# Layer norm with GELU: statistics in groups of three tiles that match the transfer blocks, one tile in three on ScalarE

## The chip, the cores and the metric

The kernel runs on one core of a Trainium2 chip. The metric is the device time of one execution in microseconds (us), and a time given for a kernel is the median of its runs. Executions of one kernel scatter by 0.5 to 2.6 us here. Comparisons are made by ratio, with a 95% interval. PE is the matrix engine, DVE VectorE, ACT ScalarE, POOL GpSimd, SP the engine whose queue issues the large transfers.

## The reference

```python
# x: (8, 1024, 2048) f32, gamma and beta: (2048,), eps = 1e-5
mean = np.mean(x, axis=-1, keepdims=True)
var = np.var(x, axis=-1, keepdims=True)
normalized = (x - mean) / np.sqrt(var + eps)
out = gamma * normalized + beta
return 0.5 * out * (1 + np.tanh(np.sqrt(2 / np.pi) * (out + 0.044715 * out ** 3)))
```

The 8192 rows are 64 tiles of 128 rows; a tile is 1.05 MB. All of x comes in once and a result of the same size goes out: 134.22 MB.

## The kernel before

Tiles travel in blocks: tile 0 alone, then 21 blocks of three tiles (3.15 MB a transfer; the first of these comes in, and the last goes out, tile by tile). Seven block buffers form a ring; the result overwrites x in its buffer. A load waits for the store that last used its buffer.

```python
starts = [0] + list(range(1, ntiles, R))          # R = 3, blocks 0 to 21
groups = [1, 1, 2] + [4] * 14 + [2, 1, 1]         # tiles that share one POOL chain
on_scalar = {first[g] for g, size in enumerate(groups) if size == 4}   # 14 tiles

def chunk(i, c):                                  # statistics of a quarter tile on DVE
    ...bn_stats; after the 4th quarter bn_aggr
def scalar_mean(i): ...                           # ACT pass over the tile, sums x
def scalar_var(i):  ...                           # ACT pass, sums (x - mean)^2; POOL scales it
def group_chain(g):                               # POOL: 1/sqrt(var + eps) by three Newton steps
    ...                                           # 15 tiny operations, each needs the one before
def diagonal(j):                                  # ACT: w = ident * std, one per tile
def affine(j):                                    # per half: DVE writes (x - mean) * gamma to PSUM,
    ...                                           # PE adds w^T beta on top (needs diagonal(j))
def gelu(j):                                      # per half: ACT gelu(PSUM / std) -> x's buffer
    ...                                           # last tile of a block: store(b), load(b + 6)

for j in range(ntiles):
    g, k = of_tile[j]
    target = min(len(chunks), max(pos + GAP, done_at[g] + SLACK))   # GAP, SLACK = 3, 7
    while pos < target:
        ...chunk(i, c)                            # where a group is complete: its chain
    if k == 0:
        for q in range(groups[g]):
            diagonal(j + q)
    affine(j)
    if j > 0:
        gelu(j - 1)
    ...                                           # then perhaps one ACT statistics pass
```

PSUM has room for two tiles' products, so `affine(j)` waits for `gelu(j - 2)`.

## Time and profile before

| before | value | how to read it |
|---|---|---|
| time | 322.51 us (322.26 to 322.91, 3 runs) | span in the profile 320.9 us |
| DVE, ACT, POOL, PE busy | 88, 67, 38, 81% | an average, not a proof of a bound |
| x in, result out on the DMA engines | 98.2% of the span | the candidate for the bound |

The waits between engines show how few of DVE's there were, and what ACT waited for. The columns are total us, times, longest; `...` marks lines left out here and below:

```profile
ACT xt L179 <- PE ps L170: 59.3, 62, 6.0
...
ACT w L161 <- POOL std L155: 26.6, 15, 5.6
DVE st L124 <- DMA xt<-in_x_dram: 18.3, 6, 4.7
...
DVE ps L167 <- ACT xt L179: 1.9, 5, 0.4
```

Only x made DVE wait noticeably; ACT waited mostly for products from PE, and in 15 places for the end of a POOL chain.

### The profile page before, as it was taken

To read this page: it belongs to the slowest core of one execution; us is meant where nothing else is said; L and a number is where in the kernel's file an instruction comes from. 1 tells how busy PE (TensorE), PEld (TensorE's weight loads), DVE (VectorE), ACT (ScalarE), POOL (GpSimd) and SP (SyncE) were. 2 spreads that over 40 slices of the span, in tenths; PEclk is the share of its full clock that TensorE was granted. 3 is DMA by queue.
4 is the path that set the end of the run, shared out by engine and by line. 5 is a ranking of instruction groups with operands and counts; after the bars stand their busy time and mean duration, and the time that the engine had idled before them with its cause. 6 is when DMAs were issued, how large, how long until landed. Compare 5 with 4: busy or idle time off the path is not lost.

```text
span 320.9 us, 2333 instructions
## 1 busy us (share of the span) xinstructions
PE 259.1 (81%) x528; PEld 102.8 (32%) x528; DVE 284.0 (88%) x379; ACT 215.7 (67%) x254; POOL 120.7 (38%) x319
## 2 busy tenths in 40 slices
PE   6988399888888888887499888748988859888990
PEld 2333144333333333333143333213333323333430
DVE  3999999999999999979499999849999979999830
ACT  3248399979787777775648787761978774655751
POOL 0771506080615334260301707030071532658840
PEclk9999869999999999997879999996999998999998
DMA  7999999999999999999999999999999999999597
GB/s 296 452 417 435 439 405 407 434 423 432 426 435 432 423 429 418 434 432 433 432 420 438 436 438 432 414 437 438 432 438 425 417 441 438 435 425 433 245 425 312
DMA packets 7074, 134.38 MB, mean 419 GB/s; under 512 B 786, under 2 KB 786, under 8 KB 1042
## 3 DMA queue, kind: packets, MB, share of 16 engines
q1 hardware_dynamic: 7056, 134.22, 98.2%
q8 instruction: 4, 0.07, 0.1%
q14 instruction: 10, 0.08, 0.1%
q10 hardware_dynamic: 4, 0.02, 0.0%
HBM read 67.13 MB, written 67.11 MB: 418 GB/s over the span
## 4 chain that ended last, share of the span: by engine, by line
DMA 49%; DVE 24%; POOL 12%; issue 8%; PE 2%; ACT 2%; POOLq 0%; SPq 0%; DVEq 0%; ACTq 0%
DMA out_dram<-xt 26%; DMA xt<-in_x_dram 23%; DVE ps L167 12%; DVE st L124 11%; POOL t L152 3%; POOL y L154 2%; POOL t L153 2%; PE ps L170 2%; POOL t L151 2%; ACT xt L179 1%; DVE mv L126 1%; POOL std L155 1%; POOL y L148 1%; POOL ve L147 1%; ACT w L161 0%
## 5 line engine op out<-in xcount | busy, mean ns | idle before, releaser
L170 PE MATMUL ps<-b_t,w 128*128 128x512 f32 x512 | 245.1, 628 | 51.6 <-DVE ps L167 43.8
L179 ACT ACTIVATE xt<-ps,y 128x1024 f32<-128x1024 f32 x128 | 139.3, 1107 | 60.0 <-PE ps L170 59.3
L170 PEld LDWEIGHTS ps<-b_t,w 128*128 128x128 f32 x512 | 97.6, 199 | 199.8 <-issue 100.9
L167 DVE SCALAR_TENSOR_TENSOR ps<-xt,mv,g_t 128x1024 f32<-128x1024 f32 x128 | 157.6, 1276 | 1.9 <-ACT xt L179 1.9
L124 DVE BATCH_NORM_STATS2 st<-xt 128x6 f32<-128x512 f32 x200 | 125.8, 672 | 18.4 <-DMA xt<-in_x_dram 18.3
L137 POOL TENSOR_SCALAR mv<-sq 128x1 f32<-128x1 f32 x14 | 3.8, 268 | 101.8 <-ACT junk L135 101.8
L161 ACT ACTIVATE w<-ident,std 128x128 f32<-128x128 f32 x64 | 20.8, 390 | 26.6 <-POOL std L155 26.6
L152 POOL TENSOR_TENSOR t<-t,ve 128x4 f32<-128x4 f32 (+2 forms) x60 | 35.3, 589 | 4.7
L147 POOL TENSOR_SCALAR ve<-mv 128x4 f32<-128x4 f32 (+2 forms) x20 | 4.6, 229 | 62.6 <-DVE mv L126 62.2
L135 ACT ACTIVATE junk<-xt,mv 128x2048 fp8e5<-128x2048 f32 x14 | 27.9, 1994 | 0.0
L153 POOL TENSOR_SCALAR t<-t 128x4 f32<-128x4 f32 (+2 forms) x60 | 25.4, 423 | 5.3
L130 ACT ACTIVATE junk<-xt 128x2048 fp8e5<-128x2048 f32 x14 | 26.6, 1901 | 0.0
L151 POOL TENSOR_TENSOR t<-y 128x4 f32<-128x4 f32 (+2 forms) x60 | 23.0, 383 | 4.8
L154 POOL TENSOR_TENSOR y<-y,t 128x4 f32<-128x4 f32 (+2 forms) x60 | 16.5, 276 | 5.0
L126 DVE BATCH_NORM_AGGREGATE mv<-st 128x2 f32<-128x24 f32 x50 | 13.2, 264 | 2.8
L97 PE MATMUL ps<-g_t,ones 1*128 1x512 f32 x8 | 7.2, 1072 | 2.6 <-DMA g_t<-in_gamma_dram 2.6
L97 PE MATMUL ps<-b_t,ones 1*128 1x512 f32 x8 | 7.0, 1056 | 0.0
L155 POOL TENSOR_TENSOR std<-ve,y 128x4 f32<-128x4 f32 (+2 forms) x20 | 5.9, 293 | 1.6
L148 POOL TENSOR_SCALAR y<-ve 128x4 int32<-128x4 int32 (+2 forms) x20 | 5.8, 289 | 1.7
L100 ACT ACTIVATE g_t<-ps 128x1024 f32<-128x1024 f32 x2 | 2.0, 1023 | 5.7 <-PE ps L97 5.7
L100 ACT ACTIVATE b_t<-ps 128x1024 f32<-128x1024 f32 x2 | 2.0, 1023 | 4.8 <-PE ps L97 4.8
L97 PEld LDWEIGHTS ps<-g_t,ones 1*128 1x128 f32 x8 | 2.5, 325 | 5.7 <-issue 5.7
(11 smaller groups left out, 10.4 us busy)
## 6 DMA issues: line engine op xcount, KB each, us to landing
xt<-in_x_dram SPq DMA_DIRECT2D x20, 3072.0 KB, 21.9
out_dram<-xt SPq DMA_DIRECT2D x20, 3072.0 KB, 27.1
xt<-in_x_dram SPq DMA_DIRECT2D x4, 1024.0 KB, 8.3
out_dram<-xt SPq DMA_DIRECT2D x3, 1024.0 KB, 18.6
out_dram<-xt SPq DMA_DIRECT2D x2, 512.0 KB, 5.5
g_t<-in_gamma_dram ACTq DMA_DIRECT2D x1, 8.0 KB
b_t<-in_beta_dram ACTq DMA_DIRECT2D x1, 8.0 KB
```

Source lines behind the costliest of these rows:

```text
L97: nc.tensor.matmul(pt[:, c:c + BANK], lhsT=ones[0:1, :], rhs=row[0:1, s.start + c:s.start + c + BANK], start=True, stop=True)
L124: nc.vector.bn_stats(out=sts[i][:, c, :], in_=xts[i][:, c * BANK:(c + 1) * BANK])
L130: nc.scalar.activation(out=junk, in_=xts[i], func=ACTF.Identity, scale=-1.0 / d, accum_out=slot(i)[:, 0:1], saturate=False)
L135: nc.scalar.activation(out=junk, in_=xts[i], func=ACTF.Square, bias=slot(i)[:, 0:1], accum_out=sq, saturate=False)
L151: po.tensor_tensor(out=t, in0=y, in1=y, op=MUL)
L152: po.tensor_tensor(out=t, in0=t, in1=ve, op=MUL)
L153: po.tensor_scalar(out=t, in0=t, scalar1=-0.5, scalar2=1.5, op0=MUL, op1=ADD)
L154: po.tensor_tensor(out=y, in0=y, in1=t, op=MUL)
L161: nc.scalar.activation(out=w, in_=ident, func=ACTF.Identity, scale=rstds[g][1][:, k:k + 1])
L167: nc.vector.scalar_tensor_tensor(out=pt, in0=xts[j][:, s], scalar=mvs[g][:, k, 0:1], in1=g_t[:, s], op0=ADD if j in on_scalar else SUB, op ...
L170: nc.tensor.matmul(pt[:, c:c + BANK], lhsT=wts[j], rhs=b_t[:, s.start + c:s.start + c + BANK], start=False, stop=True, skip_group_check=True)
L179: nc.scalar.activation(out=xts[j][:, s], in_=pt, func=ACTF.Gelu_apprx_tanh, scale=rstds[g][0][:, k:k + 1])
```

## The change

The groups become equal to the blocks, each group's first tile has its statistics on ScalarE (21 tiles instead of 14), and the distance between statistics and products is set by position in the group. This takes work off VectorE, the busiest engine, and lets a group of products end where a store begins.

```diff
-    GAP, SLACK = 3, 7
-    groups = [1, 1, 2] + [4] * 14 + [2, 1, 1]
+    groups = [1] + [3] * ((ntiles - 1) // 3)
-    on_scalar = {first[g] for g, size in enumerate(groups) if size == 4}
+    on_scalar = {first[g] for g, size in enumerate(groups) if size == 3}
+    AFTER = (6, 9, 11)
-        target = min(len(chunks), max(pos + GAP, done_at[g] + SLACK))
+        target = min(len(chunks), max(pos, done_at[g] + AFTER[k]))
-        if passes and of_tile[passes[0][1]][0] <= now and (j + 1 == ntiles or of_tile[j + 1][1]):
+        if passes and of_tile[passes[0][1]][0] <= now and k != 1:
```

## The prediction

> **What bounds the kernel now.** I read four views in this order: the busy lines and slices of the page, the DMA queue table, the waits of the queue that issues the transfers, and a table of stretches of the last 25 us.
>
> ```profile
> PE 259.1 (81%) x528; PEld 102.8 (32%) x528; DVE 284.0 (88%) x379; ACT 215.7 (67%) x254; POOL 120.7 (38%) x319
> ...
> DVE   3999999999999999979499999849999979999830
> ...
> DMA   7999999999999999999999999999999999999597
> GB/s 296 452 417 435 439 405 407 434 423 432 426 435 432 423 429 418 434 432 433 432 420 438 436 438 432 414 437 438 432 438 425 417 441 438 435 425 433 245 425 312
> ...
> q1 hardware_dynamic: 7056, 134.22, 98.2%
> ```
>
> DVE looks like the bound at 88%, but the DMA row has a 9 in every slice but four: the first, and 297 to 305 us and after. The queue that carries x in and the result out holds the 16 DMA engines 98.2% of the span. 134.22 MB must move whatever the kernel computes. The busy share of DVE is high because its work nearly fits the transfers' time, not because it sets it.
>
> ```profile
> SPq L71 <- DMA out_dram<-xt: 184.9, 15, 15.1
> SPq L187 <- ACT xt L179: 80.5, 10, 18.0
> ```
>
> The issuing queue waits 184.9 us for stores to land before it may load into their buffers (15 loads, all the later ones): the ring of seven buffers is full, and transfers, not arithmetic, pace it. From 106 to 254 us the stretch table of that time has the DMA share at 1.00 to 1.01 and 429 to 430 GB/s. Only the tail shows transfers waiting for arithmetic:
>
> ```profile
> 296.00:300.00 4.00, 4.00 (x10) 1.71 (x9) 3.84 (x4) 2.23 (x2) 3.59 (x6) 1.00 0.90 387
> 300.00:304.00 4.00, 4.00 (x11) 1.75 (x10) 3.15 (x3) 2.78 (x4) 3.51 (x7) 1.00 0.29 123
> 304.00:308.00 4.00, 4.00 (x11) 1.85 (x10) 3.04 (x3) 1.96 (x2) 3.44 (x7) 1.00 1.09 461
> 308.00:312.00 4.00, 3.34 (x8) 1.26 (x8) 0.00 (x0) 2.88 (x4) 0.76 (x4) 1.00 0.88 375
> 316.00:321.00 5.00, 0.00 (x0) 0.00 (x0) 0.00 (x0) 0.00 (x0) 0.00 (x0) 0.73 0.59 238
> ```
>
> The last two numbers of a line are DMA share and GB/s, the others busy times of PE, weight loads, DVE, ACT, POOL. From 300 to 304 us the DMA share is 0.29: the store of block 20 is issued only at 303.16 us, after the GELU of tile 60. That looks like a hole of some 3 us. But each transfer has sixteen shares, one per DMA engine, and the trace records each share's completion. The store of block 19 (3.15 MB) completes its first share at 299.82 us and its last at 304.36. The slowest share was still busy when the next store came at 303.16, so on that engine there was no hole. Its last completions are 289.87, 297.12, 304.36 (7.25 us a block), then 311.88, 314.34 and 316.88 for block 20 and tiles 61 and 62, and 319.44 for the second half of tile 63. After 304.36 a pure 7.25 us a block would give 304.36 + 2 x 7.25 = 318.86. So the visible hole of 3 us cost the slowest share only 319.44 - 318.86 = 0.6 us.
>
> **What the Trainium skill says.** "Perfetto Trace Analysis", section Roofline: a single core may pull more than its 358 GB/s share of memory, but is bounded by its 16 DMA engines at about 435 GB/s. The trace agrees: 429 to 430 GB/s over the middle, 3.1457 MB in 7.25 us = 434 GB/s on the slowest share. "DMA: Bandwidth & Descriptors", section Latency and other measured facts: some DMA engines are usually slower than the others (the cause given there is a guess, for another way of issuing). Here the completions of one block are spread by 4.5 us late in the run; which engines these are I did not find. "SBUF — State Buffer", section SBUF: two separate sides: DVE and GpSimd share a port pair as an exclusive lock, the loser waits out the instruction. The trace agrees: the same small POOL operations last 0.20 us, and about 1.1 us in many places where DVE runs the two-input product (from 291.64 to 301.14 us a chain of 15 took 9.5 us, in the quiet start 25.53 - 21.44 = 4.1 us).
>
> **The change part by part.**
>
> ```profile
> L179 ACT ACTIVATE xt<-ps,y 128x1024 f32<-128x1024 f32 x128 | 139.3, 1107 | 60.0 <-PE ps L170 59.3
> ...
> L167 DVE SCALAR_TENSOR_TENSOR ps<-xt,mv,g_t 128x1024 f32<-128x1024 f32 x128 | 157.6, 1276 | 1.9 <-ACT xt L179 1.9
> L124 DVE BATCH_NORM_STATS2 st<-xt 128x6 f32<-128x512 f32 x200 | 125.8, 672 | 18.4 <-DMA xt<-in_x_dram 18.3
> ```
>
> First figure after the bar: busy time of the group; I divide that by the count, since neighbours overlap.
>
> (1) Seven more tiles (21, not 14) have statistics on ScalarE. DVE loses 7 x (4 x 125.8/200 + 13.2/50) = 7 x 2.78 = 19.5 us: 284.0 becomes about 264.5. ACT gains 7 x (1.90 + 1.99 + 2 x 0.19 for reading the sums) = 7 x 4.28 = 30 us: 215.7 becomes about 246.
>
> (2) 22 groups instead of 20: two more POOL chains of 15 operations, 120.7/20 = 6.0 us each, and seven more scalings: POOL about 135 us, under half the span.
>
> (3) Transfers, bytes, buffers and their issue order on the queue are unchanged; the instruction listing of both kernels shows the same 38 rows there.
>
> Per block of three tiles DVE then needs 2 x 2.78 + 6 x 157.6/128 = 5.56 + 7.39 = 12.95 us (before, averaged, 13.9), ACT 6 x 1.09 + 3 x 0.33 + 4.28 = 11.8 us, PE 24 products at about 0.46 = 11.1 us. A load and a store of a block need 2 x 7.25 = 14.5 us. All engines stay below that; before they were below it too. So 19.5 us off DVE lie wholly beside transfers: DVE will wait longer for x, nothing else.
>
> (4) Start. The first 19 tiles are loaded without a condition; the slowest share ends them at 50.7 us, the store of tile 0 at 53.95. Only then (its buffer) can load 7 go out. In the new order the second store needs tile 9's first half: block 3 has landed by 28.1, and 20.8 (block 2) + 14 chunks at 0.695 + 4 products at 2.46 + about 4 us for PE and GELU = 44 us. That is before 52, so no hole; gain 0.
>
> (5) Tail. The last loads land at 260.80 and 275.33 us. In the new DVE order, after the wait at 260.8: 8 chunks, 2 aggregates and 3 products (12.95 us) to 273.8, wait to 275.3, 8 chunks, 2 aggregates and 3 products to 288.3. Tile 61's second scalar pass ends near 288.4, then one POOL chain of about 9 us instead of three in a row: 297.5, diagonals 298.5, GELU of tile 60 to about 300.7. Store 19 goes out near 286 (before 290.75), store 20 near 301 (before 303.16). Then PE paces: 3.7 us a tile after 298.3, so tiles 61, 62, 63 leave near 303, 307 and 310.5 (before 306.59, 311.49 and 314.38). The fast shares' hole shrinks to about 1 us, the slowest share has none and ends at 318.9 instead of 319.44. **Gain about 0.6 us.**
>
> Sum: 322.51 - 0.6 = **321.9 us**.
>
> **Rivals.** (a) The hole counts in full: the slowest share speeds up once others have less to do. The missing shares of 296 to 304 us are 0.1 x 4 + 0.71 x 4 = 3.2 us, with the end up to 4 us: about 318.5 us. Against it: when the fast shares stopped at 299.8, the slow one kept its 7.24 us a block. (b) A new wait: ScalarE's queue now puts the mean of a block not yet landed, and diagonals that wait for a POOL chain, ahead of the third tile's GELU, and that GELU frees the PSUM half that DVE needs. From the end of a block's statistics to the product that needs this half DVE has about 9 x 0.63 + 0.26 + 2 x 2.46 = 10.8 us; a chain under contention (8 to 9.5) with diagonals and half a GELU needs 10 to 12. If it costs 1.2 us a block DVE comes to 14.2 us, still under 14.5; if it costs 3, 15 blocks lose 1.5 us each, and the time is 345. Speaks against it: chains only take that long when DVE is not waiting, and the ring holds a block ahead. (c) DVE was the true bound: 19.5 us less would give 303 us; against it, 134.22 MB at 434 GB/s are 309 us by themselves.
>
> **Range and chances.** The three times before lie within 0.7 us. The slowest share loses some 6 us over the run in short delays I cannot attribute (one load took 8.7 us instead of 7.3 near 125 us); these may shift by 1 us either way. With (a) in part below and a little of (b) above: 320.5 to 323.3. Faster by over 2% means below 316.1, less than the transfers leave: 0.01. Slower by over 2% needs (b) at full size: 0.03. Within 2%: 0.96.
>
> **What would show it right or wrong.** Right: DVE busy near 264.5 and ACT near 246; DVE's wait for x above 30 us instead of 18.3; DMA still 9 in the middle slices and 98% or more on the queue; the share in the hole near 300 us rises from 0.29 to above 0.6, with the span shorter by less than 1.5 us. Wrong: 6s or 7s in the middle of the DMA row (rival b), products waiting for ScalarE by tens of us; or a span under 318 (rival a).

## The result, and the profile after

The changed kernel took 322.12 us (321.52 to 322.72, 4 runs) against 322.71 us (322.26 to 323.08, 4 runs) for the kernel before in the same rounds. Ratios in this document are the mean time of one kernel's runs over that of the other's in the same rounds, so not quite the ratio of the medians; here 0.9982, with a 95% interval of 0.9959 to 1.0006.

The page's busy lines and slices of the changed kernel:

```profile
PE 253.1 (79%) x528; PEld 104.0 (33%) x528; DVE 269.1 (84%) x344; ACT 238.6 (75%) x282; POOL 149.6 (47%) x356
...
DVE   2677799999999999999999999999999989798420
...
DMA   7999999999999999999999999999999999999797
GB/s 297 442 427 440 440 406 397 430 439 424 440 421 431 431 437 437 418 434 423 437 434 424 434 434 427 433 427 437 422 443 421 428 441 427 439 418 431 308 424 315
...
q1 hardware_dynamic: 7056, 134.22, 98.4%
```

DVE lost 15 us of work, ACT gained 23, and the DMA row differs from the one before in a single slice (7 instead of 5, at 297 to 305 us). The waits tell where the freed time went:

```profile
SPq L186 <- ACT xt L178: 154.0, 16, 23.6
SPq L70 <- DMA out_dram<-xt: 125.0, 14, 14.2
...
ACT w L160 <- POOL std L154: 49.9, 21, 6.4
DVE ps L166 <- ACT xt L178: 21.1, 37, 4.3
...
DVE st L123 <- DMA xt<-in_x_dram: 12.1, 5, 4.9
```

The queue now waits more for GELU results (154.0 us, before 80.5) and less for stores to land (125.0, before 184.9). DVE waits less for x, and 21.1 us for ScalarE to free PSUM, instead of 1.9. So the stores of the first half leave **later** in the changed kernel, although its busiest engine has less to do: block 2 at 61.00 us instead of 55.45, block 6 at 114.34 instead of 106.18, block 11 at 181.03 instead of 180.31. The tail, in stretches of 4 us (last two numbers: DMA share, GB/s; the others as in the prediction's table of this kind):

```profile
296.00:300.00 4.00, 1.42 (x4) 0.39 (x3) 0.62 (x1) 1.08 (x4) 2.23 (x9) 1.00 0.89 381
300.00:304.00 4.00, 4.00 (x11) 1.81 (x10) 3.06 (x3) 3.80 (x4) 0.00 (x0) 1.00 0.64 270
304.00:308.00 4.00, 4.00 (x10) 1.71 (x9) 1.82 (x2) 2.46 (x3) 0.00 (x0) 1.00 0.95 406
308.00:312.00 4.00, 1.94 (x5) 0.57 (x3) 0.00 (x0) 2.23 (x2) 0.00 (x0) 1.00 0.95 399
```

In the hole at 300 to 304 us the DMA share rose from 0.29 to 0.64, yet the end moved by only 1.2 us in this pair of profiles.

**A new loop.** ACT's and POOL's instructions in order of time (start, duration, engine and line; in brackets the idle time before, and what ended it) show one block period of the changed kernel. First POOL, the beginning of a chain, its end, and the next beginning:

```profile
129.72 0.22 POOL L136 TENSOR_SCALAR mv<-sq 128x1 f32<-128x1 f32 x1 [5.09 <-ACT junk L134]
...
137.77 0.20 POOL L154 TENSOR_TENSOR std<-ve,y 128x3 f32<-128x3 f32 x1
143.06 0.22 POOL L136 TENSOR_SCALAR mv<-sq 128x1 f32<-128x1 f32 x1 [5.09 <-ACT junk L134]
```

Then ACT between the two chains:

```profile
138.00 0.98 ACT L160 ACTIVATE w<-ident,std 128x128 f32<-128x128 f32 x3 [2.46 <-POOL std L154]
138.89 2.10 ACT L178 ACTIVATE xt<-ps,y 128x1024 f32<-128x1024 f32 x2
140.89 1.99 ACT L134 ACTIVATE junk<-xt,mv 128x2048 fp8e5<-128x2048 f32 x1
142.78 0.19 ACT L134 ACTIVATION_READ_ACCUMULATOR junk<-xt,mv 128x1 f32 x1
```

A chain ends (137.97). ACT makes the diagonals that waited for it, then the GELU behind them in its order, then the variance pass of the next block; only that lets the next chain begin. 8.25 (chain, with the scaling of the variance in front) + 0.03 + 0.89 (diagonals) + 2.00 (GELU) + 2.08 (variance) + 0.09 = 13.34 us, and 143.06 - 129.72 = 13.34. The stores of blocks 2 to 10 are issued at 61.00, 74.34, 87.67, 101.01, 114.34, 127.68, 141.01, 154.35 and 167.69 us: the same 13.34 us apart. The loop, not VectorE and not yet the transfers, paces the stores there; from 194 to 253 us each store goes out right behind a load, 14.5 to 15.0 us apart; by 261.04 us (block 17) the stores are back on the loop's count. The DMA engines do not run dry in all this (share 1.00 from 61 to 254 us), since the ring holds work ahead.

The questions for the experiments were therefore three. Do the transfers alone explain the time? How near is this loop to costing time? And where do the 0.6 us come from?

### The profile page after: what moved, and what is told of

It is laid out like the page before. It is cut to its first block, busy times and chain, and to the rows that moved or that the text cites. A ratio compares the mean times of both kernels' runs of the same rounds, so it can differ in the third digit from the quotient of the medians.

```text
span 319.7 us, 2374 instructions
## 1 busy us (share of the span) xinstructions
PE 253.1 (79%) x528; PEld 104.0 (33%) x528; DVE 269.1 (84%) x344; ACT 238.6 (75%) x282; POOL 149.6 (47%) x356
## 3 DMA queue, kind: packets, MB, share of 16 engines
q1 hardware_dynamic: 7056, 134.22, 98.4%
## 4 chain that ended last, share of the span: by engine, by line
DMA 34%; POOL 30%; issue 26%; PE 3%; ACT 2%; DVE 1%; POOLq 0%; SPq 0%; ACTq 0%
DMA out_dram<-xt 26%; POOL t L152 10%; DMA xt<-in_x_dram 8%; POOL y L153 6%; POOL t L151 6%; PE ps L169 3%; POOL t L150 3%; ACT xt L178 2%; POOL mv L136 1%; POOL std L154 1%; POOL ve L146 1%; DVE st L123 1%; POOL y L147 1%; ACT w L160 1%; DVE ps L166 0%
## 5 line engine op out<-in xcount | busy, mean ns | idle before, releaser
L169 PE MATMUL ps<-b_t,w 128*128 128x512 f32 x512 | 239.1, 625 | 53.3 <-ACT w L160 52.4
L166 DVE SCALAR_TENSOR_TENSOR ps<-xt,mv,g_t 128x1024 f32<-128x1024 f32 x128 | 158.7, 1287 | 21.1 <-ACT xt L178 21.1
L178 ACT ACTIVATE xt<-ps,y 128x1024 f32<-128x1024 f32 x128 | 134.4, 1107 | 9.6 <-PE ps L169 8.9
L123 DVE BATCH_NORM_STATS2 st<-xt 128x6 f32<-128x512 f32 x172 | 109.5, 670 | 12.1 <-DMA xt<-in_x_dram 12.1
L160 ACT ACTIVATE w<-ident,std 128x128 f32<-128x128 f32 x64 | 21.1, 391 | 49.9 <-POOL std L154 49.9
L152 POOL TENSOR_SCALAR t<-t 128x3 f32<-128x3 f32 (+1 forms) x66 | 50.7, 767 | 5.8
L134 ACT ACTIVATE junk<-xt,mv 128x2048 fp8e5<-128x2048 f32 x21 | 41.9, 1993 | 0.1
L129 ACT ACTIVATE junk<-xt 128x2048 fp8e5<-128x2048 f32 x21 | 40.2, 1916 | 0.0
L153 POOL TENSOR_TENSOR y<-y,t 128x3 f32<-128x3 f32 (+1 forms) x66 | 32.2, 488 | 5.5
L151 POOL TENSOR_TENSOR t<-t,ve 128x3 f32<-128x3 f32 (+1 forms) x66 | 31.2, 473 | 5.2
L150 POOL TENSOR_TENSOR t<-y 128x3 f32<-128x3 f32 (+1 forms) x66 | 14.8, 224 | 5.3
L146 POOL TENSOR_SCALAR ve<-mv 128x3 f32<-128x3 f32 (+1 forms) x22 | 5.2, 235 | 9.1 <-DVE mv L125 7.4
L154 POOL TENSOR_TENSOR std<-ve,y 128x3 f32<-128x3 f32 (+1 forms) x22 | 5.2, 237 | 1.7
(11 smaller groups left out, 13.4 us busy)
```

The source lines that it names most:

```text
L123: nc.vector.bn_stats(out=sts[i][:, c, :], in_=xts[i][:, c * BANK:(c + 1) * BANK])
L129: nc.scalar.activation(out=junk, in_=xts[i], func=ACTF.Identity, scale=-1.0 / d, accum_out=slot(i)[:, 0:1], saturate=False)
L134: nc.scalar.activation(out=junk, in_=xts[i], func=ACTF.Square, bias=slot(i)[:, 0:1], accum_out=sq, saturate=False)
L150: po.tensor_tensor(out=t, in0=y, in1=y, op=MUL)
L151: po.tensor_tensor(out=t, in0=t, in1=ve, op=MUL)
L152: po.tensor_scalar(out=t, in0=t, scalar1=-0.5, scalar2=1.5, op0=MUL, op1=ADD)
```

## The experiments

Twelve runs, all correct but the first, which is wrong. Each ratio is to the kernel before, run in the same rounds. The difference shown is against the changed kernel unless said. "Store 20" is the store of block 20, the last full block, as its issue time in the trace.

### 1. Transfers alone

The loop over the tiles is replaced by the loads and stores in the same order on the same queue, as soon as data and buffers allow.

```diff
-    for j in range(ntiles):
-        ...  (statistics, products, GELU, stores)
+    for j in range(ntiles):
+        store(j)          # the same stores; after store(b) the load of block b + 6
```

> All loads and stores of the changed kernel, in the same queue, order and sizes, with no statistics, products or GELU on the tiles (the result is x itself, wrong on purpose). Theory (the slowest of the 16 DMA shares sets the end): 320.5 to 322.5 us, within 0.5% of both kernels, last shares of the blocks about 7.25 us apart. Rival (arithmetic still costs some us through waits for buffers or late stores): below 318 us.

Measured: 321.63 us (320.63 to 322.51), ratio to before 0.9967 (0.9946 to 0.9989). The page of this run:

```profile
PE 14.0 (4%) x16; PEld 5.1 (2%) x16; DVE 0.2 (0%) x1; ACT 5.6 (2%) x6; POOL 0.5 (0%) x5
...
DMA   7999999999999999999999999999999999999993
...
q1 hardware_dynamic: 7056, 134.22, 98.1%
```

With 0.2 us of VectorE work the kernel takes the same time to 0.3%. This is the floor of the transfers as they are arranged; the kernel before stands 0.3% above it (interval 0.1 to 0.5%), the changed kernel 0.1 to 0.2%, which is within the scatter. The spread between the first and last share of a block is there too (block 19: first share complete at 299.33 us, last at 303.96), so it does not come from the arithmetic.

### 2. A store in the tail sent earlier

```diff
+        early = k == 0 and g == len(groups) - 1
+        if early:
+            gelu(j - 1)               # tile 60, ahead of the last diagonals
         if k == 0: ...diagonals
-        if j > 0:
+        if j > 0 and not early:
             gelu(j - 1)
```

> The changed kernel with one move in the tail: the GELU of tile 60 comes ahead of the last group's diagonals on ScalarE, so the store of block 20 is issued near 297 to 298 us instead of 301.94. Theory (the slowest share alone counts, and it had no hole): DMA share 300 to 304 us rises from 0.64 to 0.8 or more, time as the changed kernel within 0.3 us (321.8 to 322.4). Rival (the hole counts in full for all shares): 2 to 3 us less, about 319.5 us.

Measured: 322.29 us, ratio 0.9987 (0.9970 to 1.0004). Store 20 left at 297.38 us, and the stretch table of its tail has the hole at 300 us filled:

```profile
296.00:300.00 4.00, 0.20 (x1) 0.00 (x0) 2.52 (x3) 1.11 (x1) 3.35 (x9) 0.79 0.97 418
300.00:304.00 4.00, 3.42 (x4) 1.50 (x5) 0.00 (x0) 0.99 (x3) 0.10 (x1) 0.50 1.00 430
304.00:308.00 4.00, 4.00 (x9) 1.73 (x8) 1.57 (x2) 2.23 (x2) 0.00 (x0) 0.86 0.81 350
308.00:312.00 4.00, 4.00 (x11) 1.76 (x10) 1.01 (x1) 2.50 (x3) 0.00 (x0) 1.00 0.74 307
```

The share at 300 to 304 us is 1.00 instead of 0.64 and the time did not fall; block 20's slowest share ended at 311.48 us here against 310.85 in the changed kernel's profile. But the hole has moved to 304 to 312 us rather than closed: from 296 to 312 us the missing shares add up to 1.9 us, in the changed kernel to 2.3. So this run alone does not rule out that the hole counts in full; runs 1 and 7, which have none, do.

### 3. Only the tail undone

```diff
-    groups = [1] + [3] * ((ntiles - 1) // 3)
+    groups = [1] + [3] * 20 + [1, 1, 1]
```

> The changed kernel with only its tail undone: tiles 61, 62 and 63 are three groups with one chain each and all statistics on VectorE, as before. Theory: the gain of the change sits in the tail, so this gives it back: the last half tile's store is issued near 314 us instead of 311.1, and the time is 0.3 to 1 us above the changed kernel (322.4 to 323.1). Rival (the gain is chance in the middle of the run): the same as the changed kernel, 322.1 within 0.2 us.

Measured: 321.94 us, ratio 0.9980 (0.9960 to 1.0000); the same as the changed kernel. The last store did leave late, at 315.12 us (near 314 expected), and it gave nothing back that can be measured. But this edit does not restore the old tail: tile 61's chain now stands alone, and the store of block 20 left at 299.34 us, not at 303.16 as in the kernel before or at 301.94 as in the changed one. So the run shows that a late last store costs nothing; it does not test whether the late store 20 of the kernel before did.

### 4 and 5. A longer chain, in both kernels

```diff
-        for _ in range(3):            # in group_chain
+        for _ in range(5):
```

> The changed kernel with five steps of the inverse square root instead of three: eight more operations in each POOL chain, nothing else. Theory (a loop of chain, diagonals, one GELU and the next variance pass, 13.34 us a block, runs just below the 14.5 us of a block's transfers): the loop grows by 8 operations of 0.28 to 0.6 us to 15.6 to 18 us a block, above the transfers, and the time to 350 to 390 us, with the stores issued at that spacing. Rival (the chain is hidden beside VectorE's 12.95 us and the transfers): 322 to 326 us, only the tail later.

> The kernel before with five steps of the inverse square root instead of three. Theory: the same loop exists there, but once per four tiles: about 8.3 us of chain, 1.3 of diagonals, 2.1 of GELU, 2.2 of variance pass, 14 us against 19.4 us of transfers for four tiles; with 2.2 to 5 us more it stays below, so the middle keeps its pace and only the tail's three chains are later: 323 to 330 us. Rival (a longer chain hurts both kernels alike): as the changed kernel with five steps, 350 us or more.

Measured: the changed kernel 366.87 us, ratio 1.1368 (1.1347 to 1.1390); the kernel before 339.25 us, ratio 1.0526 (1.0508 to 1.0543). The first hit the theory: a chain of 10.4 us instead of 8.25 and stores 15.53 us apart (15.6 to 18 expected). The second missed its range of 323 to 330 us, though the loop there did stay below the transfers: chains began at 150.97, 169.47 and 187.98 us, 18.5 us per four tiles against 19.4 (13.9 per three tiles against 14.5). A loop below the transfers' pace was not enough. That led to the next theory, and to run 9.

### 6. The longer chain with the loop cut

```diff
-        for _ in range(3):
+        for _ in range(5):
...
-        if passes and of_tile[passes[0][1]][0] <= now and k != 1:
-            f, q = passes.pop(0)
-            f(q)
+        for _ in range(2 if k == 2 else 0):      # mean and variance pass back to back,
+            if passes and of_tile[passes[0][1]][0] <= now:      # ahead of the diagonals
+                f, q = passes.pop(0)
+                f(q)
```

> The changed kernel with five steps, and the variance pass of a block put right behind its mean pass on ScalarE, ahead of the previous block's diagonals and GELU. That cuts the loop: a chain no longer waits for what the chain before released. Theory: the spacing of the stores falls from 15.6 to 18 us to the larger of VectorE's 13 us, ScalarE's 12 us and POOL's own chain (11 to 13 us), below the transfers' 14.5: time 322 to 327 us. Rival (the longer chain itself is what costs, not the loop): within 2% of the changed kernel with five steps alone.

Measured: 331.48 us, ratio 1.0279 (1.0241 to 1.0318). 35 of the 45 us came back by moving one pass, so the loop, not the chain's length by itself, was most of the cost. But it is above the expected 322 to 327 us: the stores are still 13.7 us apart, and the first block's leaves at 52.00 us instead of 47.66.

### 7. A shorter chain

```diff
-        for _ in range(3):
+        for _ in range(1):
```

> The changed kernel with one step instead of three (the inverse root is less exact, on purpose): eight operations fewer in each chain. Theory: the loop shrinks to 9 to 11 us, the product's waits for ScalarE on VectorE (21.1 us) fall below 8 us, VectorE's wait for x grows from 12 to over 25 us, and the time stays at 321.5 to 322.5 us since transfers set it. Rival (the loop costs time before the ring of buffers is full): below 319 us.

Measured: 322.41 us, ratio 0.9999 (0.9982 to 1.0015). DVE's waits in this run:

```profile
DVE st L123 <- DMA xt<-in_x_dram: 29.5, 14, 4.6
...
DVE ps L166 <- ACT xt L178: 3.4, 2, 2.1
```

With the loop this much shorter the wait for ScalarE turns into a wait for x, and no time is won. In the changed kernel the loop costs nothing that these runs can measure. The tail of this run has no hole either: from 296 to 312 us its DMA shares are 0.93, 1.07, 0.92 and 1.00.

```profile
300.00:304.00 4.00, 4.00 (x11) 1.77 (x10) 3.20 (x3) 2.59 (x4) 0.00 (x0) 1.00 1.07 455
304.00:308.00 4.00, 3.32 (x8) 1.14 (x6) 0.00 (x0) 2.79 (x3) 0.00 (x0) 1.00 0.92 393
```

So closing the hole all but some 0.3 us is worth no measurable time, which rules out that it counts in full.

### 8. All statistics on VectorE

```diff
-    on_scalar = {first[g] for g, size in enumerate(groups) if size == 3}
+    on_scalar = {first[g] for g, size in enumerate(groups) if size == 0}
```

> The changed kernel with no statistics on ScalarE: all 64 tiles on VectorE. Theory: VectorE then needs 3 x 2.78 + 7.39 = 15.7 us a block, above 14.5, and sets the time: 21 x 15.7 plus about 15 us of start and end = 340 to 350 us, VectorE busy above 95%. Rival (VectorE's share has no bearing at all): 322 to 325 us.

Measured: 356.76 us, ratio 1.1062 (1.1045 to 1.1078); 7 us above the expected range, and DVE was 90% busy, not over 95%. The stores were at first 15.1 us apart, later 15.1 and 15.6 in turn. With groups of three, statistics on ScalarE are needed; how few tiles would do was not tried.

### 9. One step more: a loop just below the transfers

```diff
-        for _ in range(3):
+        for _ in range(4):
```

> The changed kernel with four steps of the inverse square root: four more operations in each chain. Three and five steps gave stores 13.34 and 15.53 us apart, so four give about 14.4 us, below the 14.5 us of a block's load and store. Theory A (what counts is the sum: first block's store plus 19 spacings must reach the store of block 20 by about 302 us, which allows only (302.3 - 47.7) / 19 = 13.4 us a block, since the last five blocks have no loads between their stores): store 20 near 50 + 19 x 14.4 = 324 us and the time near 343 us. Theory B (as predicted: a loop below 14.5 us a block is hidden): 322 to 324 us.

Measured: 343.63 us, ratio 1.0638 (1.0612 to 1.0664). Theory A hit, theory B is out by 20 us. The slices and the end of the issuing queue (start, then the time from the first to the last issue of the row):

```profile
DMA   8999999999999999999999999999999978346297
GB/s 298 451 431 414 452 371 446 418 440 422 426 443 420 428 426 424 437 417 424 437 423 434 434 403 449 423 431 431 418 443 423 440 329 345 166 205 276 92 419 318
```

```profile
252.14 0.33 SPq L186 DMA_DIRECT2D out_dram<-xt  x1
255.14 0.34 SPq L70 DMA_DIRECT2D xt<-in_x_dram  x1
266.58 57.90 SPq L186 DMA_DIRECT2D out_dram<-xt  x5
```

The middle is as full as in the fast kernels. The loss stands at the end, where the loads have run out: five stores are issued over 57.90 us, 14.4 us apart, while each takes the DMA engines 7.25 us.

### 10. The loop cut, with three steps

The reorder of run 6 without the longer chain.

> The changed kernel with three steps and the variance pass right behind the mean pass, which cuts the loop of chains. Theory A: spacing falls from 13.34 to about 12.9 us (VectorE), the ring of buffers is full before 150 us instead of 194, VectorE's waits for ScalarE fall, and the time stays at 321.6 to 322.6 us since transfers alone took 321.6. Rival (the loop costs the changed kernel something): 320.5 us or less, below the transfers-only run.

Measured: 322.78 us, ratio 1.0010 (0.9985 to 1.0034). The rival is out, and the time is 0.2 us above theory A's range, within the scatter. The spacing is not as it says: 13.5 us on average (12.65 and 14.34 in turn), not 12.9. Two passes in a row on ACT now delay the diagonals in every second block, and DVE waits 1.5 us there. Two more of its signs failed: VectorE's waits for ScalarE rose to 24.3 us, and loads hold the stores back only after 200 us, not before 150. With five steps the spacing was 13.7, of the same two values, so the chain's length hardly counts any more, but the reorder does not speed the stores.

### 11. Less lead of the statistics

```diff
-    AFTER = (6, 9, 11)
+    AFTER = (3, 6, 8)
```

> The changed kernel with the products three chunks nearer to the statistics (3, 6 and 8 chunks beyond the group's own instead of 6, 9 and 11), so about one tile less lead. Theory A: the next chain can then start only after a product that waits for the GELU that the chain before released; the loop becomes 8.3 + 0.9 + 2.0 + 2.5 + 1.5 = 15 us a block, above the 13.4 us allowed, and the time 345 to 358 us. Rival (the lead has no bearing while transfers bound it): 322 to 323 us.

Measured: 335.19 us, ratio 1.0384 (1.0363 to 1.0406). The direction is theory A's and the rival is out; the size is below the range, as stores are 14.1 us apart, not 15. The next chain's first group operation waited for DVE's statistics (POOL idle 0.88 us there); my sum counted a whole GELU where the product waits for half of one. The longer distance between statistics and products is a needed part of the change.

### 12. The changed kernel again

No edit.

> The changed kernel itself once more, with more rounds, to see whether its 0.2% gain is real. Theory of the prediction (0.6 us from the tail): ratio 0.997 to 0.999 with an interval below 1. Rival (the gain is within the scatter of the transfers): ratio 0.999 to 1.001, interval across 1.

Measured: 321.86 us (321.29 to 322.34), ratio 0.9972 (0.9953 to 0.9991). Here the interval excludes 1, in the first comparison (0.9982) it did not: the gain is small, some 0.1 to 0.5%, and the transfers-only run had no more to offer. No version was clearly faster than the changed kernel.

### The sum that decides

A store that finds its engines idle lands its first share 8.5 us after its issue (store 20 of the changed kernel: 301.94 to 310.47), of which some 7.2 us move data. The slowest share of block 19 was done at 303.60, so store 20 must be issued by about 303.60 - 1.3 = 302.3 us (an estimate from this one trace), or the end moves. The path of arithmetic reaches store 20 at: issue of store 1, plus 19 spacings.

| run | store 1 | spacing, us | store 1 + 19 spacings | store 20 | 322.0 + lateness over 302.3 | time |
|---|---|---|---|---|---|---|
| changed kernel | 47.66 | 13.34 | 301.1 | 301.94 | 322.0 | 322.12 |
| 10, loop cut | 47.77 | 13.50 | 304.3 | 303.25 | 323.0 | 322.78 |
| 6, five steps, loop cut | 52.00 | 13.67 | 311.7 | 310.74 | 330.4 | 331.48 |
| 11, less lead | 46.57 | 14.12 | 314.8 | 314.83 | 334.5 | 335.19 |
| 9, four steps | 50.07 | 14.43 | 324.3 | 324.14 | 343.8 | 343.63 |
| 8, all on VectorE | 45.64 | 15.25 | 335.3 | 336.85 | 356.6 | 356.76 |
| 4, five steps | 51.95 | 15.54 | 347.2 | 347.09 | 366.8 | 366.87 |

Spacings are means from store 1 to store 16 (to store 10 or 11 in the first two rows, before loads hold the stores back). The 322.0 is set by the changed kernel; the other six fall on the line within about 1 us. The sum works out to a limit of (302.3 - 47.7) / 19 = 13.4 us a block, not the 14.5 us of a block's load and store, since the last five stores have no loads between them. The changed kernel, at 13.34, stands just inside. The kernel before with five steps agrees in part: its 13.9 us per three tiles is above 13.4, store 20 left at 314.63, 12.3 us late, and its three longer tail chains put its last store at 333.03 us; it lost 16.7 us.

## Why the prediction was right or wrong

**The bound: right.** 98.2% on the queue was the bound. Transfers alone took 321.63 us, and a kernel with eight operations fewer per chain 322.41. The forecast of rival (c), 303 us, is out by the result and by the first run. One reading was off: the DMA row of the kernel before has three slices below 9, not four; and the slow chain that was timed at 9.5 us ran from 291.64 to 301.33, which is 9.7.

**The time and the size: right, its source shown in part.** 321.9 us predicted, 322.12 and 321.86 measured. Step (5) put the 0.6 us into the tail. Its issue times came out within 1.3 us but for store 19 (286 predicted, 288.75 measured): stores 20, 61, 62 and the last at 301.94, 304.25, 307.69 and 311.12, and the slowest share ended at 318.24 (318.9 predicted). Runs 2 and 3 do not decide it, since neither has the late store 20 of the kernel before. The completion records of the traces say more. From the last share of block 19 to the last of all, the kernel before took 15.08 us, with store 20 issued at 303.16. The changed kernel took 14.64 and 14.68 (run 12), and runs 1, 2, 3 and 7, all with store 20 issued before 302 us, 14.64 to 14.67; run 10, with store 20 at 303.25, took 15.21. So some 0.4 us of the 0.6 are seen in the tail, though in a single trace of the kernel before. The rest is not shown: block 19's last share itself comes anywhere from 303.60 to 305.46 us in these traces, which is more than the whole gain.

**Rival (a): right to reject.** Run 7 had no hole and no gain (322.41 us).

**Part (1), the sizes: DVE off by 5 us, ACT by 7.** DVE measured 269.1 (264.5 predicted): a quarter's statistics took 109.5/172 = 0.637 us of busy time instead of 0.629, and the products 158.7 us instead of 157.6, together 2.4 us; the rest is overlap of neighbours, which the sum over groups counts twice (12.6 us before, 10.4 now). ACT measured 238.6 (246): GELUs run back to back now overlap more, 134.4 us for 128 instead of 139.3, which is most of it. POOL measured 149.6 (135): its chains cost 6.8 us each, not 6.0.

**The step that failed: "So 19.5 us off DVE lie wholly beside transfers: DVE will wait longer for x, nothing else."** It waited less for x (12.1 us; above 30 predicted) and 21.1 us for ScalarE. I had compared the busy sums of single engines (12.95 us for DVE) with 14.5 us, and overlooked that chain, diagonals, GELU and variance pass form a loop across ACT and POOL that no busy sum shows. Rival (b) had the right engines, and guessed 1.2 us a block beyond 12.95; 13.34 - 12.95 = 0.4 us is what it came to. I also wrote that it would still be hidden below 14.5 us. That limit was wrong: the runs put it near 13.4. That the forecast held is in this part luck, because the loop came out 0.06 us a block inside that limit; at 14.4 us, which I had called hidden, the time is 343.63 us (run 9).

**The start.** Step (4) put the second store near 44 us; it left at 47.66. That opened no hole, as forecast, but it is the start from which the 13.4 us are counted.

**What would show it right or wrong:** the DMA share near 300 us rose to 0.64 (above 0.6 predicted), the queue kept 98.4%, the middle of the DMA row kept its 9s, and the span fell by 1.2 us (less than 1.5 predicted). But DVE's longer wait for x did not come, and one sign named for being wrong did: products waited 21.1 us for ScalarE.

## What to carry to other kernels

Where transfers bound a kernel, run it once without arithmetic: that is the floor, and it tells at once whether a lighter engine can win anything. Do not compare each engine's busy time per block with the transfers' time per block; find the serial loop across engines from the spacing of the stores, and check start + blocks x spacing against the moment when the last store is due, because the stores at the end have no loads to hide behind. A change that costs nothing can still use up the slack: with two Newton steps more the changed kernel lost 45 us, the kernel before 17.

## What the Trainium skill lacked or had wrong

- "DMA: Bandwidth & Descriptors", section Where 436 GB/s comes from, says without a condition that for transfers between HBM and SBUF the HBM side (about 358 GB/s) binds, though it quotes 425 GB/s for a large one in the next sentence. The transfers-only run moved 134.24 MB at a mean of 420 GB/s over the whole span, loads and stores mixed, and 430 to 431 in the middle. "Perfetto Trace Analysis", section Roofline, has it right: a single active core is bounded by its 16 DMA engines near 435.
- "DMA: Bandwidth & Descriptors", section Latency and other measured facts, names slower DMA engines and calls it specific to descriptors written by GpSimd. Here all large transfers are issued by the SP queue, and the completions of one block still lie 4.2 us (changed kernel, 299.43 to 303.60) to 4.6 us (transfers alone) apart. Which engines lag, and why, no run here shows; no page gives the size of such a spread.
- "Perfetto Trace Analysis", section What "DMA-bound" means, gives no test for how much delay of the arithmetic a transfer-bound kernel still tolerates. Here 14.4 us of arithmetic per block under 14.5 us of transfers cost 21 us, and 13.34 us cost none.
- "SBUF — State Buffer", section SBUF: two separate sides, states the lock between DVE and GpSimd, and this agrees (small POOL operations 0.20 us, or about 1.1 us beside DVE's products). No page gives what such waits cost a serial chain: 15 operations took 4.1 us in quiet and 8 to 9.7 us beside the products, and here that sits in the loop that paces the stores.
